# A GLA mixer with a convolutional FFN on one core: state tiles of their own, the first block's heads a unit later, token sums moved to the last block, the last LayerNorm read back inside the FFN, and a reordered opening

## Chip, cores and metric

One core of a Trainium2 chip runs the whole kernel. The metric is device time in microseconds (us) of one execution; lower is better. The kernel before takes 2162.0 us, the median of 3 runs (2158.67 to 2163.49).

## What is computed

One decoder layer of the reference: a chunked gated linear attention (GLA) mixer, then a causal ConvFFN, each with a residual, a LayerNorm and an adaLN modulation from the conditioning vector c. S = 2048 tokens, D = 1024, 4 heads of 128 key and 256 value columns, 2816 hidden columns in the FFN. All is float32.

```python
mod = silu(c) @ mod_w + mod_b                     # shift, scale, gate of each sub-layer
h = x * (1 + scale) + shift
q, k, v, r, a_lr = split(h @ w_in)                # GLA
b = cumsum(log_sigmoid(a_lr @ w_a2 + b_a) / 16)   # in chunks of 64 tokens
o = causal(q_dec @ k_inv.T) @ v + q_dec @ state   # per chunk
state = state * exp(b_last) + k_dec.T @ v
o = o * rsqrt(mean(o * o) + eps) * norm_g
x = layer_norm(alpha * x + gate * ((o * silu(r)) @ w_o))
h = x * (1 + scale2) + shift2
x = layer_norm(alpha * x + gate2 * (convffn(h) @ w_down))
```

## The kernel before, in words

Every float32 product is made from three float32r products: an operand is split into a high part (a cast on ACT, L104) and a rest (a subtraction on DVE, L107), and `mm3` issues high x high, high x rest, rest x high (L110, L111, L112). These three lines are nearly all of TensorE's (PE's) work.

The mixer runs over four blocks of 512 tokens (tb 0 to 3). A block is 32 *units*; a unit is one 1 MB split weight tile `hl` and 24 matmuls of 512 columns. Units 0 to 3 make v for heads 0 and 1, 4 to 7 q and k of these heads, 8 to 11 the gate r; 12 to 23 repeat this for heads 2 and 3; 24 to 31 are the output projection. Weights come as `raw` loads on the SP queue and are split two units ahead, some are stored split (`wq_d`) and loaded back in later blocks. In the last block all come split, so neither ACT nor DVE has a weight to split there.

The rest of the mixer is cut into steps that `at_unit` hangs on a unit and `tick` runs in the order in which they were hung. A head has four: `head_a` (four transposes of k, L635, evicted as `KTt`; then two banks of `ps_w<-Q,KI` attention products, read by DVE's masked copies L649, L650), `head_b` (state updates: products into a bank, DVE's L676 or L678 into `S32[:, h]`, split into `Shl`), `head_c` (output products `v,at` and `Shl,Q` into two banks of 12 matmuls each; ACT squares L704, POOL's power L170/L171, ACT's `on` L710 reads the bank again), `head_d` (transposes L718 and the gate L720). Before, the registering loops put all `head_a` ahead of `head_c`, so that where both hang on one unit (head 1's a with head 0's c, head 3's a with head 2's c) a comes first. Each head's state lives in one slice of one tile, so that the next update of a head overwrites what the split of the last one reads.

PSUM has eight banks: four under the tag "mm" for the long products (`ps_mm`) and four under "w" (`ps_w`), taken in turn by every head step, transpose group and small product. A matmul into a bank waits until its last reader there is done.

Three further places are touched. The **opening**: PE spins on a constant tile (L400; 62, 4 and 18 matmuls) while the modulation sums run (eight rows, 0 to 7, accumulated on DVE, L226/L231; row 7 of the first pair on ACT, L239, and PE, L242; `mod_fin`, L253 to L258), until `make` (L518, L520) has the first modulated x split into `xm`. `x_pre` (L284 to L298) loads four 512 KB tiles, makes four differences of token quarters for the FFN's seven Strassen-like products and stores them; it is called twice in tb 2 for the first half of the tokens (units 4 and 13) and twice in the FFN for the second (steps 6 and 9). The **hand-off** to the FFN: the last block's normalised rows `z` (L778) stay in SBUF as `zs_last`, and `start_rest` transposes all of them (32 transposes, L759, evicted by ACT as `xt`, L764) between the products of FFN step 0. The FFN then has 2 x 22 steps of seven products each, and a down-projection follows. In step 0 the third product adds to the bank of the first, which ACT must have copied out as `p1` (L948) before.

## Time and profile before

| | |
|---|---|
| median of 3 runs | 2162.0 us |
| the profiled execution | 2164.01 us |
| its span | 2162.3 us |
| busy: PE, DVE, ACT, POOL | 99%, 67%, 41%, 6% |
| chain that ended last | PE 92%, DVE 3%, ACT 2%, DMA 2%, issue 1% |
| granted TensorE clock, mean | 0.994 |

How to read it: PE's busy share is an average over the span, and its rest is the waits that the view of waits lists by releaser. A matmul is pipelined, so its own duration overlaps the next one's; the step from start to start is what it costs. The granted clock is 1.00 or 0.50 of full speed in a stretch (2.4 or 1.2 GHz).

### The profile page before, as it was taken

What the parts mean: (1) busy time and instruction counts of PE and PEld (TensorE: products, weight loads), DVE (VectorE), ACT (ScalarE), POOL (GpSimd) and SP (SyncE); (2) the same over time, 40 slices, a digit from 0 to 9 for tenths busy, and PEclk for the clock granted to TensorE, in tenths of its full rate; (3) what the DMA queues carried; (4) which work ended last, traced back from release to release, by engine and by line L of the source; (5) the groups of instructions that cost most, each with busy time, mean ns of one, the idle gap of its engine ahead of it and who ended that gap; (6) DMA issues with size and microseconds to landing.
All of it is one profiled execution on the core that took longest, in us unless ns stands there. A gap on an engine that the chain in (4) does not pass through costs nothing.

```text
span 2162.3 us, 26743 instructions
## 1 busy us (share of the span) xinstructions
PE 2135.5 (99%) x9924; PEld 1780.3 (82%) x9924; DVE 1456.6 (67%) x2031; ACT 886.2 (41%) x1333; POOL 134.5 (6%) x298
## 2 busy tenths in 40 slices
PE   9899999999999999999999999999999999999998
PEld 8788888888888888788888888888888888888887
DVE  6788666667443444688777778766666797578556
ACT  3545443443342333544444445333333443344333
POOL 0111101010001000100000000000000000021002
PEclk9999999999999999999999999999999999999999
DMA  7387547589756546687545558877777797577562
GB/s 298 120 286 287 172 176 265 205 315 359 252 195 246 187 166 230 247 324 275 185 178 204 182 194 319 311 251 275 259 266 264 269 327 278 185 240 258 193 204 88
DMA packets 150211, 515.66 MB, mean 238 GB/s; under 512 B 17120, under 2 KB 17248, under 8 KB 132160
## 3 DMA queue, kind: packets, MB, share of 16 engines
q1 hardware_dynamic: 150080, 513.94, 66.7%
q8 instruction: 78, 1.28, 0.2%
q14 instruction: 53, 0.43, 0.1%
HBM read 351.09 MB, written 162.79 MB: 238 GB/s over the span
## 4 chain that ended last, share of the span: by engine, by line
PE 92%; DVE 3%; ACT 2%; DMA 2%; issue 1%; POOL 0%; SPq 0%; DVEq 0%; POOLq 0%; ACTq 0%
PE ps_mm L110 22%; PE ps_mm L112 22%; PE ps_mm L111 22%; PE ps_w L110 8%; PE ps_w L111 8%; PE ps_w L112 8%; DMA xs<-xt_d 1%; PE ps_w L400 1%; PE ps_w L718 1%; DMA raw<-in_wab_dram 1%; PE ps_w L759 0%; DVE hl L107 0%; PE ps_w L487 0%; ACT hl L104 0%; PE ps_w L488 0%
## 5 line engine op out<-in xcount | busy, mean ns | idle before, releaser
L110 PE MATMUL ps_mm<-xc,hl 128*128 128x512 f32 x704 | 274.3, 390 | 1.7 <-ACT p L948 1.0
L112 PE MATMUL ps_mm<-xc,hl 128*128 128x512 f32 x704 | 274.0, 389 | 0.2 <-DVE hl L107 0.2
L111 PE MATMUL ps_mm<-xc,hl 128*128 128x512 f32 x704 | 273.8, 389 | 0.0
L110 PE MATMUL ps_mm<-xm,hl 128*128 128x512 f32 x496 | 195.1, 393 | 0.3 <-ACT hl L104 0.3
L112 PE MATMUL ps_mm<-xm,hl 128*128 128x512 f32 x496 | 193.6, 390 | 1.6 <-DVE hl L107 1.6
L111 PE MATMUL ps_mm<-xm,hl 128*128 128x512 f32 x496 | 193.7, 391 | 0.0
L110 PEld LDWEIGHTS ps_mm<-xc,hl 128*128 128x128 f32 x704 | 132.1, 188 | 30.1 <-ACT p L948 1.7
L112 PEld LDWEIGHTS ps_mm<-xc,hl 128*128 128x128 f32 x704 | 132.1, 188 | 28.0 <-DVE hl L107 0.6
L111 PEld LDWEIGHTS ps_mm<-xc,hl 128*128 128x128 f32 x704 | 132.1, 188 | 27.3
L962 DVE SCALAR_TENSOR_TENSOR ct<-U,cw_sb,ct 128x512 f32<-128x512 f32 x176 | 131.7, 748 | 19.2 <-ACT ct L956 17.7
L104 ACT CAST hl<-raw 128x1024 fp32r<-128x1024 f32 (+1 forms) x91 | 89.5, 983 | 130.8 <-PE ps_mm L112 54.3
L107 DVE TENSOR_TENSOR hl<-raw,hl 128x1024 fp32r<-128x1024 f32 (+1 forms) x91 | 103.4, 1138 | 56.7 <-ACT hl L104 56.2
L110 PE MATMUL ps_w<-xc,hl 128*128 128x512 f32 x352 | 137.0, 389 | 0.4 <-ACT xt L764 0.4
L111 PE MATMUL ps_w<-xc,hl 128*128 128x512 f32 x352 | 136.9, 389 | 0.0
L112 PE MATMUL ps_w<-xc,hl 128*128 128x512 f32 x352 | 136.9, 389 | 0.0
L104 ACT CAST dhl<-raw 128x1024 fp32r<-128x1024 f32 x57 | 60.1, 1054 | 163.7 <-PE ps_mm L112 103.2
L107 DVE TENSOR_TENSOR dhl<-raw,dhl 128x1024 fp32r<-128x1024 f32 x57 | 69.6, 1221 | 69.4 <-ACT dhl L104 69.4
L112 PEld LDWEIGHTS ps_mm<-xm,hl 128*128 128x128 f32 x496 | 93.3, 188 | 21.7 <-DVE hl L107 2.0
L110 PEld LDWEIGHTS ps_mm<-xm,hl 128*128 128x128 f32 x496 | 93.5, 189 | 19.1 <-ACT hl L104 0.8
L111 PEld LDWEIGHTS ps_mm<-xm,hl 128*128 128x128 f32 x496 | 93.4, 188 | 17.9
L110 PE MATMUL ps_mm<-dhl 128*128 128x512 f32 x264 | 102.7, 389 | 0.0
L111 PE MATMUL ps_mm<-dhl 128*128 128x512 f32 x264 | 102.7, 389 | 0.0
(239 smaller groups left out, 4979.0 us busy)
## 6 DMA issues: line engine op xcount, KB each, us to landing
hl<-wq_d SPq DMA_DIRECT2D x64, 1024.0 KB, 4.8
hc_d<-ct SPq DMA_DIRECT2D x154, 256.0 KB, 2.6
raw<-hc_d SPq DMA_DIRECT2D x70, 512.0 KB, 4.3
draw<-wc_d SPq DMA_DIRECT2D x70, 512.0 KB, 4.9
raw<-in_wab_dram SPq DMA_DIRECT2D x64, 512.0 KB, 5.2
wq_d<-hl SPq DMA_DIRECT2D x32, 1024.0 KB, 4.9
wu<-in_wup_dram SPq DMA_DIRECT2D x44, 512.0 KB, 4.3
wg<-in_wup_dram SPq DMA_DIRECT2D x44, 512.0 KB, 3.6
```

Source lines behind the costliest of these rows:

```text
L104: accs["copy"] = nc.scalar.copy(h, src)
L107: return nc.vector.tensor_tensor(l, src if lsrc is None else lsrc, h.bitcast(F32), op=ALU.subtract)
L110: nc.tensor.matmul(po, a[0], b[0], start=first, stop=False, skip_group_check=resumed)
L111: nc.tensor.matmul(po, a[0], b[1], start=False, stop=False, skip_group_check=resumed)
L112: return nc.tensor.matmul(po, a[1], b[0], start=False, stop=last, skip_group_check=resumed)
L400: mm = nc.tensor.matmul(pm[:, 256:512], still[:, 0:P], still, start=True, stop=True)
L718: nc.tensor.transpose(pt[:, s * P:s * P + P], on[:, s, e * P:e * P + P], ident)
L962: nc.vector.scalar_tensor_tensor(ct, U[:, o + i:o + i + 512], cw_sb[:, j, i:i + 1], ct, op0=ALU.mult, op1=ALU.add)
```

## The change

- **State tiles.** Each state update writes a tile of its own out of eight (tag "S"), not the head's slice of `S32`.
- **Heads.** In tb 0 all head steps come one unit later. One loop now hangs all four steps of a head, so that in every block `head_c` of head 0 comes ahead of `head_a` of head 1 in their common unit, and the same for heads 2 and 3.
- **Modulation sums** of the second sub-layer: the same 16 pieces in tb 0, six of the last seven one to three units later; `mod2` at unit 28.
- **x_pre** of the first half: from tb 2 (units 4, 13) to tb 3 (units 3, 14); the first one of the second half from FFN step 6 to 7.
- **Last LayerNorm.** `start_rest` makes no transposes. Step 1 of the FFN loads the four stored tiles `z` again, steps 2 to 5 transpose and evict two column groups each.
- **Opening.** Spins of 64 and 13 in a bank of their own; all eight rows of the first sum on DVE; both first weight casts ahead of the first `xraw` on ACT; ACT makes row 0 of the later sums; `waw` in one copy and one subtraction.

```diff
@@ -28,7 +28,7 @@
 HALF = 1024
 NP = NJ // 2
 AHEAD = 2
-SPIN = (62, 4, 18)
+SPIN = (64, 13)
 KEEP = [2] * 10 + [1] * 4 + [0] * 10 + [1] * 8
 ALPHA = 2.0 ** 0.25
 EPS = 1e-5
@@ -207,7 +207,11 @@
     def mod_row(raws, dk):
         return raws[dk // 2].rearrange("p (k d c) -> p k d c", k=2, d=2)[:, :, dk % 2]
 
-    def mod_cols(s, pr, qs, raws=None, by_act=False, after=None, rows=range(KT)):
+    def mod_row1(s, pr, raws, after):
+        accs[s, pr] = t2p.tile([P, 2, 256], F32, tag="t2", name="macc")
+        order(nc.scalar.activation(accs[s, pr], mod_row(raws, 0), AF.Copy, scale=cs[:, 0:1]), after)
+
+    def mod_cols(s, pr, qs, raws=None, rows=range(KT), after=None):
         if raws is None:
             raws = {}
             for q in qs:
@@ -220,42 +224,21 @@
             sc = cs[:, dk:dk + 1]
             if dk == 0:
                 accs[s, pr] = t2p.tile([P, 2, 256], F32, tag="t2", name="macc")
-                if by_act:
-                    order(nc.scalar.activation(accs[s, pr], wk, AF.Copy, scale=sc), after[0])
-                else:
-                    i = nc.vector.tensor_scalar(accs[s, pr], wk, sc, None, op0=ALU.mult)
-                    if after is not None:
-                        order(i, after[1])
+                i = nc.vector.tensor_scalar(accs[s, pr], wk, sc, None, op0=ALU.mult)
             else:
                 acc = accs[s, pr]
-                accs["last"] = nc.vector.scalar_tensor_tensor(acc, wk, sc, acc, op0=ALU.mult, op1=ALU.add)
-                if dk == 1 and by_act:
-                    order(accs["last"], accs["hl"])
-
...
-    def mod_fin(s, pr, pm=None):
+                i = accs["last"] = nc.vector.scalar_tensor_tensor(acc, wk, sc, acc, op0=ALU.mult, op1=ALU.add)
+            if after is not None:
+                order(i, after)
+                after = None
+
+    def mod_fin(s, pr):
         acc = accs.pop((s, pr))
-        o = md[:, s, 2 * pr:2 * pr + 2]
-        b = mbs_sb[:, s, 2 * pr:2 * pr + 2]
-        if pm is None:
-            pm = psum("w", 4)
-        else:
-            i = nc.vector.tensor_tensor(o, pm[:, 4:8].rearrange("p (k c) -> p k c", k=2), b, op=ALU.add)
-            order(i, accs["last"])
-            b = o
+        pm = psum("w", 4)
         for c in range(4):
             mm = nc.tensor.matmul(pm[:, c:c + 1], acc[:, c // 2, c % 2 * P:c % 2 * P + P], one, start=True, stop=True)
-        return mm, nc.vector.tensor_tensor(o, pm[:, 0:4].rearrange("p (k c) -> p k c", k=2), b, op=ALU.add)
+        return mm, nc.vector.tensor_tensor(md[:, s, 2 * pr:2 * pr + 2], pm[:, 0:4].rearrange("p (k c) -> p k c", k=2),
+                                           mbs_sb[:, s, 2 * pr:2 * pr + 2], op=ALU.add)
 
...
-        pm0 = psum("w", 4)
-        spin(SPIN[0], pm0)
-        mod_cols(0, 0, range(4), start[0][0], rows=range(7))
-        acc_last = accs["last"]
-        spin(SPIN[1], pm0, mod_rows_act(start[0][0], (7,), pm0))
+        ps_spin = psum("mm", 4)
+        spin(SPIN[0], ps_spin)
+        mod_cols(0, 0, range(4), start[0][0])
 
         load(ba_sb, ba)
         load(ng_sb, ng)
         waw = ab.tile([P, KT, 96], F32R, name="waw")
 
         def make_waw(after):
-            for r in range(3):
-                order(nc.scalar.copy(waw[:, :, r * 32:r * 32 + 16], war), after)
-                nc.vector.tensor_tensor(waw[:, :, r * 32 + 16:r * 32 + 32], war,
-                                        waw[:, :, r * 32:r * 32 + 16].bitcast(F32), op=ALU.subtract)
+            wv = waw.rearrange("p k (r c) -> p k r c", r=3)
+            wb = war[:, :, None, :].to_broadcast([P, KT, 3, 16])
+            order(nc.scalar.copy(wv[:, :, :, 0:16], wb), after)
+            nc.vector.tensor_tensor(wv[:, :, :, 16:32], wb, wv[:, :, :, 0:16].bitcast(F32), op=ALU.subtract)
 
...
-        S32 = ab.tile([P, NH, DV], F32, name="S32")
+        state = [None] * NH
         Shl = [None] * NH
 
         def mod2():
@@ -505,43 +486,45 @@
 
             xm = []
 
-            def acc(pr):
-                mod_cols(0, pr, range(4), start[pr][0], pr == 1, (done[0], done[1 if pr == 1 else 2]))
-
-            def make(pr):
-                mm, i = mod_fin(0, pr, pm0 if pr == 0 else None)
+            def make(pr, then=None):
+                mm, i = mod_fin(0, pr)
                 if pr == 0:
-                    spin(SPIN[2], pm0, mm)
+                    order(i, accs["hl"])
+                    spin(SPIN[1], ps_spin, mm)
                 for kt in (2 * pr, 2 * pr + 1):
                     r = start[pr][1][:, kt % 2 * 512:kt % 2 * 512 + 512]
                     if kt == 1:
-                        nc.vector.tensor_scalar(r, r, md[:, 0, kt, 1:2], md[:, 0, kt, 0:1], op0=ALU.mult, op1=ALU.add)
+                        i = nc.vector.tensor_scalar(r, r, md[:, 0, kt, 1:2], md[:, 0, kt, 0:1], op0=ALU.mult, op1=ALU.add)
                     else:
                         nc.scalar.activation(r, r, AF.Identity, bias=md[:, 0, kt, 0:1], scale=md[:, 0, kt, 1:2])
+                    if kt == 1:
+                        fw.append(unit())
+                        order(accs["hl"], i)
                     t = act_tile("xm")
                     sub = split(t[:, 0], t[:, 1], r)
                     xm.append(t)
-                return accs["copy"], sub, i
+                return sub
 
             fw.append(unit())
             done = make(0)
-            accs["last"] = done[1]
-            fw.append(unit())
-            make_waw(done[1])
+            mod_row1(0, 1, start[1][0], accs["copy"])
+            accs["last"] = done
+            make_waw(done)
             issue(3)
             for pr in range(4):
                 if pr < 3:
                     load_unit()
                     if pr < 2:
                         start_loads(pr + 2)
-                    acc(pr + 1)
+                        mod_row1(0, pr + 2, start[pr + 2][0], accs["copy"])
+                    mod_cols(0, pr + 1, range(4), start[pr + 1][0], range(1, KT), accs["hl"] if pr == 0 else mod_done)
+                    mod_done = accs["last"]
                 for po, w in ((pq, fw[0]), (pk, fw[1])):
                     wv = w.rearrange("p s (k c) -> p s k c", k=KT)
                     for kt in (2 * pr, 2 * pr + 1):
                         mm3(po, (wv[:, 0, kt], wv[:, 1, kt]), (xm[kt][:, 0], xm[kt][:, 1]), kt == 0, kt == KT - 1)
                 if pr < 3:
-                    done = make(pr + 1)
-                    accs["last"] = done[1]
+                    accs["last"] = make(pr + 1)
                 mm_a(pa, xm, (2 * pr, 2 * pr + 1))
                 if pr == 2:
                     make_w2s()
@@ -672,13 +655,14 @@
                     if H["last"] and s == 3:
                         continue
                     po = pst[:, i * DV:i * DV + DV]
-                    if H["S"][s] is None:
-                        nc.vector.tensor_copy(S32[:, h], po)
+                    old, new = state[h], ab.tile([P, DV], F32, tag="S", name="S", bufs=8)
+                    if old is None:
+                        nc.vector.tensor_copy(new, po)
                     else:
-                        nc.vector.scalar_tensor_tensor(S32[:, h], S32[:, h], el[:, 1, s:s + 1], po,
-                                                       op0=ALU.mult, op1=ALU.add)
+                        nc.vector.scalar_tensor_tensor(new, old, el[:, 1, s:s + 1], po, op0=ALU.mult, op1=ALU.add)
+                    state[h] = new
                     st1 = ab.tile([P, 2, DV], F32R, tag="Shl", name="Shl", bufs=8)
-                    split(st1[:, 0], st1[:, 1], S32[:, h])
+                    split(st1[:, 0], st1[:, 1], new)
                     Shl[h] = st1
                     if i == 0:
                         H["S"][-1] = st1
@@ -752,15 +736,13 @@
                     store(zn_d[tb * 4 + t], zs[t])
             tick()
 
-        def ln1_out(tb, zs, kts, after=None):
+        def ln1_out(tb, zs, kts, by_act=False):
             for kt in kts:
                 pt = psum("w", 4)
                 for t in range(4):
-                    tr = nc.tensor.transpose(pt[:, t * P:t * P + P], zs[t][:, kt * P:kt * P + P], ident)
-                    if after is not None:
-                        order(tr, after)
+                    nc.tensor.transpose(pt[:, t * P:t * P + P], zs[t][:, kt * P:kt * P + P], ident)
                 xt = t2p.tile([P, TB], F32, tag="t2", name="xt")
-                if after is not None:
+                if by_act:
                     nc.scalar.activation(xt, pt, AF.Identity, bias=B2[:, kt:kt + 1], scale=A2[:, kt:kt + 1])
                 else:
                     nc.vector.tensor_scalar(xt, pt, A2[:, kt:kt + 1], B2[:, kt:kt + 1], op0=ALU.mult, op1=ALU.add)
@@ -803,30 +785,27 @@
             gated = []
             Hs = [dict(h=h, last=last, gated=gated) for h in range(NH)]
             for i, u in ((0, 6), (1, 8), (2, 18), (3, 20)):
-                at_unit(b + u, head_a, Hs[i])
-                at_unit(b + u + 1, head_b, Hs[i])
-            for i, u in ((0, 8), (1, 10), (2, 20), (3, 22)):
-                at_unit(b + u, head_c, Hs[i])
-            for i, u in ((0, 10), (1, 12), (2, 22), (3, 24)):
-                at_unit(b + u, head_d, Hs[i])
+                u += b + (tb == 0)
+                for k, f in ((0, head_a), (1, head_b), (2, head_c), (4, head_d)):
+                    at_unit(u + k, f, Hs[i])
             at_unit(b + 12, next_decays, (2, 3))
             if tb == 0:
                 load(lnc, lncol)
                 for k in range(8):
                     at_unit(8 + k, gate_step, 0, k, gs1)
                 at_unit(16, gate_end, 0, G1, gs1)
-                for i, u in enumerate((14, 14, 15, 15, 16, 16, 16, 17, 17, 18, 19, 20, 21, 22, 23, 24)):
+                for i, u in enumerate((14, 14, 15, 15, 16, 16, 16, 17, 17, 17, 18, 21, 23, 24, 25, 26)):
                     at_unit(u, mod_cols, 1, i // 4, (i % 4,))
                     if i % 4 == 3:
                         at_unit(u + 1, mod_fin, 1, i // 4)
-                at_unit(26, mod2)
+                at_unit(28, mod2)
...
-            if tb == 2:
-                at_unit(b + 4, x_pre, 0, 0)
-                at_unit(b + 13, x_pre, 0, 1)
+            if tb == 3:
+                at_unit(b + 3, x_pre, 0, 0)
+                at_unit(b + 14, x_pre, 0, 1)
...
-            if last:
-                zs_last = zs
-            else:
+            if not last:
                 xm = nxt["xm"]
...
-        def start_rest(last_mm):
-            ln1_out(NTB - 1, zs_last, range(8), last_mm)
+        def start_rest():
             for i in (3, 2):
                 x_fill(ur, X0, i, x_stage(up, 0, i))
 
         nextx, ahead_x = list(PROD), []
-        todo = {6: [(x_pre, 1, 0)], 9: [(x_pre, 1, 1)]}
+        zl = []
+
+        def ln1_last(n):
+            if n == 0:
+                for t in range(4):
+                    zl.append(z_tile())
+                    load(zl[-1], zn_d[4 * (NTB - 1) + t])
+            else:
+                ln1_out(NTB - 1, zl, range(2 * n - 2, 2 * n), True)
+
+        todo = {n + 1: [(ln1_last, n)] for n in range(5)} | {7: [(x_pre, 1, 0)], 9: [(x_pre, 1, 1)]}
         G2 = gp.tile([P, D], F32, tag="G", name="G2")
         load(G2, G2_d)
         prev = None
@@ -1089,7 +1075,7 @@
             else:
                 nc.gpsimd.tensor_copy(U[:, 0:2], halo[:, j])
             if n == 0:
-                start_rest(mm)
+                start_rest()
             add(nc.vector, U[:, 2:514], pb, p1)
             st["h0"] = conv_a(U, 0, j)
             if Wn is not None:
```

How the order changes, at three places. First PE in tb 1 where head 1's `head_a` and head 0's `head_c` share a unit (rows of the same kind cut; `KI_2829` of before and `KI_2828` of the change are the same tile). Before:

```order
L635 MATMUL ps_w<-ident,KI_2829 128x128 x4
L110 MATMUL ps_w<-Q,KI 128x192
L111 MATMUL ps_w<-Q,KI 128x192
L112 MATMUL ps_w<-Q,KI 128x192
L110 MATMUL ps_w<-v,at 128x256
L111 MATMUL ps_w<-v,at 128x256
L112 MATMUL ps_w<-v,at 128x256
L110 MATMUL ps_w<-Shl,Q 128x256
```

Now:

```order
L110 MATMUL ps_w<-v,at 128x256
L111 MATMUL ps_w<-v,at 128x256
L112 MATMUL ps_w<-v,at 128x256
L110 MATMUL ps_w<-Shl,Q 128x256
L111 MATMUL ps_w<-Shl,Q 128x256
L112 MATMUL ps_w<-Shl,Q 128x256
L618 MATMUL ps_w<-ident,KI_2828 128x128 x4
L110 MATMUL ps_w<-Q,KI 128x192
```

The 24 output products of head 0 now stand right ahead of head 1's transposes and its attention products, in the same turn of the four "w" banks.

Second, DVE at the state updates of head 3 in tb 0. Before:

```order
L678 SCALAR_TENSOR_TENSOR S_400<-S_400,el,ps_w 128x256
L231 SCALAR_TENSOR_TENSOR macc<-mraw,cs,macc 128x512
L107 TENSOR_TENSOR Shl<-S_400,Shl 128x256
L374 TENSOR_TENSOR raw<-raw,G_279 128x1024
L678 SCALAR_TENSOR_TENSOR S_400<-S_400,el,ps_w 128x256
```

Now:

```order
L660 COPY S<-ps_w 128x256
L240 TENSOR_TENSOR md<-ps_w,mbs_sb 128x4
L662 SCALAR_TENSOR_TENSOR S<-S,el,ps_w 128x256
L107 TENSOR_TENSOR Shl<-S,Shl 128x256
L662 SCALAR_TENSOR_TENSOR S<-S,el,ps_w 128x256
```

An update no longer stands behind the subtraction of the one before it with other work between them, and the `macc` and `raw` work left this place.

Third, ACT at the hand-off (`z` are the last block's rows, `p` and `u` the copies of the first products). Before:

```order
L778 ACTIVATE z<-z,rs 128x1024 x2
L104 CAST hl<-wu 128x1024
L104 CAST xc<-xs 128x512 x2
L948 COPY p_7731<-ps_mm 128x512
L104 CAST hl<-wg 128x1024
L764 ACTIVATE xt<-ps_w,B_107,A_106 128x512 x3
```

Now:

```order
L760 ACTIVATE z<-z,rs 128x1024 x2
L104 CAST hl<-wu 128x1024
L104 CAST xc<-xs 128x512 x2
L925 COPY p_7774<-ps_mm 128x512
L104 CAST hl<-wg 128x1024
L104 CAST hl<-wu 128x1024
L925 COPY u_7837<-ps_mm 128x512
```

What stands ahead of `p` is the same; the evictions `xt` behind it are gone from here, and on PE so are the 32 transposes (L759).

## Rows read from the trace of the kernel before

**Rows 1.** The page, part 1 (busy us, share, instructions of each engine).

```profile
PE 2135.5 (99%) x9924; PEld 1780.3 (82%) x9924; DVE 1456.6 (67%) x2031; ACT 886.2 (41%) x1333; POOL 134.5 (6%) x298
```

**Rows 2.** Waits of PE: what waited, releaser, us in all, times, longest.

```profile
PE ps_w L110 <- DVE S L678: 6.5, 3, 3.0
...
PE ps_mm L110 <- ACT u L948: 1.9, 3, 0.7
...
PE ps_w L110 <- DVE KTt L107: 0.6, 1, 0.6
```

**Rows 3.** Windows: us, busy us (xcount) of PE, PEld, DVE, ACT, POOL, PEclk, DMA, GB/s.

```profile
14.00:20.80 6.80, 6.54 (x27) 5.98 (x26) 5.43 (x10) 5.17 (x9) 0.00 (x0) 0.50 1.05 401
31.05:34.46 3.41, 3.31 (x8) 2.40 (x9) 3.41 (x5) 1.51 (x3) 0.00 (x0) 0.50 1.05 407
89.08:95.90 6.82, 5.70 (x24) 5.54 (x25) 6.14 (x12) 3.60 (x10) 1.91 (x2) 0.50 0.39 136
177.82:181.24 3.42, 3.42 (x18) 3.42 (x18) 3.22 (x7) 1.48 (x6) 0.46 (x1) 0.50 0.84 323
700.00:860.00 160.00, 160.00 (x825) 136.59 (x824) 68.25 (x120) 55.24 (x119) 9.38 (x22) 1.00 0.52 192
886.00:930.00 44.00, 39.55 (x182) 30.88 (x181) 31.46 (x45) 29.33 (x38) 5.59 (x14) 1.00 0.84 304
```

**Rows 4.** Timeline of PE: start, us, line, operation, [idle before <- releaser].

```profile
18.66 0.63 PE L110 MATMUL ps_w<-xm,hl 128*128 128x512 f32 x1
...
86.29 0.35 PE L110 MATMUL ps_w<-Q,KI 128*128 128x192 f32 x1 [1.71 <-DVE S L678]
...
90.20 0.55 PE L110 MATMUL ps_w<-v,at 128*128 128x256 f32 x1 [2.99 <-DVE S L678]
...
177.56 0.38 PE L110 MATMUL ps_w<-v,at 128*128 128x256 f32 x1 [1.85 <-DVE S L678]
...
511.35 0.50 PE L112 MATMUL ps_mm<-xm,hl 128*128 128x512 f32 x1 [1.60 <-DVE hl L107]
```

**Rows 5.** Opening: SP's second weight load, ACT rows; DMA part of 0:32 (last, landing).

```profile
5.65 0.43 SPq L125 DMA_DIRECT2D raw<-in_wab_dram  x1
...
11.28 1.05 ACT L104 CAST hl<-raw 128x1024 fp32r<-128x1024 f32 x1 [0.45 <-DMA raw<-in_wab_dram]
...
14.64 0.81 ACT L520 ACTIVATE xraw<-xraw,md 128x512 f32<-128x512 f32 x1 [2.31 <-DVE md L258]
...
raw<-in_wab_dram SPq DMA_DIRECT2D x7, 512.0 KB, 8.1
```

**Rows 6.** Timelines around a head_c: ACT, POOL and PE in tb 2; POOL in tb 0.

```profile
625.26 0.38 ACT L704 ACTIVATE sq<-ps_w 128x256 f32<-128x256 f32 x1 [0.83 <-PE ps_w L112]
...
627.37 0.84 ACT L710 ACTIVATE on<-ps_w,ss 128x256 f32<-128x256 f32 x2 [1.13 <-POOL ss L171]
...
626.63 0.71 POOL L171 TENSOR_TENSOR ss<-ss,mhalf 128x2 f32<-128x2 f32 x1
...
623.63 0.28 PE L110 MATMUL ps_w<-v,at 128*128 128x256 f32 x1
...
626.50 1.04 PE L718 MATMUL ps_w<-ident,on 128*128 128x128 f32 x8
...
93.97 1.60 POOL L171 TENSOR_TENSOR ss<-ss,mhalf 128x2 f32<-128x2 f32 x1
```

**Rows 7.** Timeline of DVE: the four differences of x_pre in tb 2.

```profile
504.50 5.00 DVE L290 TENSOR_TENSOR xp<-xp 128x1024 f32<-128x1024 f32 x4
```

**Rows 8.** Timelines at the hand-off: ACT, then PE.

```profile
895.96 0.57 ACT L948 COPY p<-ps_mm 128x512 f32<-128x512 f32 x1
...
891.64 0.39 PE L112 MATMUL ps_mm<-xc,hl 128*128 128x512 f32 x1
...
894.13 1.64 PE L759 MATMUL ps_w<-ident,z 128*128 128x128 f32 x13 [1.18 <-ACT z L778]
...
896.59 0.50 PE L110 MATMUL ps_mm<-xc,hl 128*128 128x512 f32 x1 [0.82 <-ACT p L948]
```

More of the change, by code (lines that the diff above doesn't have):

```diff
@@ L230, in mod_cols @@
                 acc = accs[s, pr]
-                accs["last"] = nc.vector.scalar_tensor_tensor(acc, wk, sc, acc, op0=ALU.mult, op1=ALU.add)
-                if dk == 1 and by_act:
-                    order(accs["last"], accs["hl"])
-    def mod_rows_act(raws, rows, pm):
-        parts = []
-        for dk in rows:
-            parts.append(t2p.tile([P, 2, 256], F32, tag="t2", name="mpart"))
-            nc.scalar.activation(parts[-1], mod_row(raws, dk), AF.Copy, scale=cs[:, dk:dk + 1])
-        for c in range(4):
-            for n, part in enumerate(parts):
-                mm = nc.tensor.matmul(pm[:, 4 + c:5 + c], part[:, c // 2, c % 2 * P:c % 2 * P + P], one,
-                                      start=n == 0, stop=n == len(parts) - 1)
-        return mm
```

## The prediction

> **What bounds the kernel now.** Read the page's part 1 first: PE is busy in 99% of the span [rows 1], so the kernel is bound by PE, and DVE, ACT and POOL matter only where PE waits for one of them. That leaves two sources of a gain, the 27 us in which PE is not busy and the stretches at half clock. So the view of PE's waits comes next [rows 2]: the reader is to see how small the list is, and that its largest entry, 6.5 us in three waits, is DVE's state update L678. Third, the windows [rows 3]: 0.50 in the clock column marks four stretches at half clock (1.2 GHz), of 6.80, 3.41, 6.82 and 3.42 us; a stretch busy with matmuls loses half its length there. Last, PE's timeline gives each wait its place [rows 4]. Some 27 us of waits and about half of 20.5 us at half clock are all that can be won; whatever the change moves on DVE, ACT or SP outside these places costs nothing as long as PE has its operands.
>
> The sum is made against the profiled execution, 2164.0 us, which lies 2.0 us above the median shown; the forecast is brought to the median at the end. Two times closer than 0.2% (4.3 us) can't be told apart here.
>
> **Opening.** Before, the first real matmul starts at 18.66 [rows 4], behind `xraw` on ACT at 14.64, which waited for the two-step `md` [rows 5]. Now ACT does both weight casts first. The second weight load is issued at 5.65 and takes 8.1 us by the median of these loads, so it lands near 13.75; a cast takes 1.05 (11.28 row), so `xraw` starts near 14.8, ends at 15.6 by its 0.81, and the first cast of `xm` lets PE start near 16.2: 2.45 us earlier [rows 5]. How much of it is worth something hangs on the clock: it is 0.50 up to 20.80 [rows 3], and if it stays so, matmuls in the 2.45 us gained run at half speed, worth 1.25. Bounds: 0.8 (the load lands half a microsecond late) and 2.45 (the clock rises as much earlier as the real work starts). Nothing here tells the two apart, and I take the middle, **-1.8**. The 3.41 us at half clock from 31.05 on, and the wait for `xm` there, stay, because the DMA share there is 1.05 [rows 3]: loads set that place, and none is removed.
>
> **Heads of tb 0 and the state tiles.** The three waits for L678 are 1.71, 2.99 and 1.85 us, 6.55 together, and the first matmul behind a wait lasts longer as the pipeline refills (0.50 at 511.35 [rows 4] against 0.39 at 891.64 [rows 8]), so some 0.1 more each, 6.9 in all. With tiles of its own an update needs only its bank and the last state, no longer the subtraction that reads the old slice; with the steps a unit later it also has left the `macc` work. I take all three as gone: -6.9. Two half-clock stretches lie around them [rows 3]. In 89.08 to 95.90 PE is busy 5.70 us at half speed, so half of it, 2.85, comes back less a little at the edges, where the pipeline hides some, 2.7; in 177.82 to 181.24 half of 3.42, 1.7. In all -6.9 - 2.7 - 1.7 = **-11.3**. The smaller end is -6.9 (the clock falls all the same).
>
> **What the new order of the steps adds.** The rows on PE's order show that head 0's 24 output products now stand right ahead of head 1's transposes and attention products. In turn they take banks po0, po1, transposes, attention 0, attention 1 out of four, so attention 1 needs po0's bank, and that is free only when ACT's `on` has read it. The chain after po0's last matmul is square, POOL power, `on`: from 625.26 to 628.21 (627.37 + 0.84), 2.95 us [rows 6]. PE fills it with 12 matmuls of 256 columns (half of the 24 between 623.63 and 626.50, 1.44 us), four transposes (half of the eight up to 627.29, 0.4) and six short products (at most 0.12 each, 0.7), less the pipeline's overlap about 2.3 us. The rest, **0.7 us**, is a new wait, at each of seven places (two in each of tb 0, 2 and 3, one in tb 1; in the other pair of tb 1 ten long matmuls stand between). At three places it is longer. Head 1 of tb 0 is the first POOL power of the program, 1.60 us at 93.97 where the one at 626.63 takes 0.71 [rows 6], and part of a weight cast stands between: 0.7 + 0.9 + 0.8 = 2.4, and 1.0 more as the clock may fall. Where a weight cast (1.05 [rows 5]) stands between the squares it is 0.7 + 0.95 = 1.65 (tb 1); in tb 0's second pair the cast is only in part in the way, 0.9. Sum: 2.4 + 1.0 + 0.9 + 1.65 + 4 x 0.7 = **+8.75**. Below, it is nothing if ACT is quicker; above, each place has the 1.60 us power. Behind a waiting `on`, ACT's next casts queue, and the `Shl` casts of the next head wait with them; these are needed two units later.
>
> **Moved pieces.** The later modulation sums hold raw tiles longer, and the weight load behind them comes later: +0.5 (0 to 2). `x_pre` leaves tb 2: DVE's four differences fill 504.50 to 509.50 [rows 7], and PE then waits 1.60 us for the weight split queued behind them [rows 4]; with the wait for `KTt` close behind it (0.6 [rows 2]) and 0.1 each of refill, **-2.4**. In tb 3 the same 5 us stand in a block without weight splits, where DVE is busy 68 of 160 us [rows 3]: +0.5 (0 to 2); the eight loads on SP are behind pre-split weights there, two units ahead. The small waits of tb 1 are left as they are.
>
> **Hand-off.** Before, PE fills the wait for `p`, from 891.9 (the last product starts at 891.64) to 896.59 [rows 8], with 16 of the 32 transposes, 1.75 us at 0.11 each (1.64 for 13, with the drain); the rest of the 4.7 is wait. What ACT has ahead of `p` (895.96) is unchanged, so now PE stands still until 896.6: **4.5 us in one piece** less the pipeline's end. The 16 transposes are paid later: +1.75. Gone are waits behind them for `u`, 1.9 [rows 2], and refill and a few tenths for `xt`: the whole window has 44.00 - 39.55 = 4.45 us without PE [rows 3], of which some 2.4 lie ahead of 896.59, so 2.05 and six refills of 0.1, -2.6. After an idle of 1.85 us at 177.56 [rows 4] a half-clock stretch of 3.42 us followed [rows 3], so one is taken here too: +1.7. Sum **+0.85**; bounds -1 (the clock holds) and +4 (two such stretches, and the waits for `u` stay in part). Before, the idle pieces here were short and the window's clock is 1.00 [rows 3].
>
> The Trainium skill, "TensorE: Matmul & The Clock Gate", section "Why this matters for your kernels", says to leave no longer idle between bursts of matmuls, else the engine falls back to half rate. By that rule the hand-off is where this change loses, and the trace agrees in its row at 177.56, so the 1.7 us stay in the sum; were the rule left out and the clock held, the sum would be 1.7 lower.
>
> **Sum.** -1.8 - 11.3 + 8.75 + 0.5 - 2.4 + 0.5 + 0.85 = -4.9, so 2159.1 for a profiled execution like this one, and 2.0 less against the median: **2157.1 us**, about 0.2% faster.
>
> **Rivals.**
>
> *The new order is free.* If the square-power-on chain ends before PE comes back to the bank (ACT idle at that point, as at 625.26), the 8.75 us are not paid: 2157.1 - 8.75 = 2148.4. For it: the surplus is only 0.7 us of 2.95 at four of the seven places. Against it: three places have a cast or the long power in the chain.
>
> *The bank wait takes the place of the state wait (the other side).* With the 1.60 us power at every place, the chain is 3.85 us and each wait 1.6; an idle of that kind can halve the clock for 3.42 us, 1.7 lost. Seven times 3.3 is 23.1 in place of 8.75: 2171.5. With the clock falling at half of the places it is 2165.5. It decides from about 0.7 us more per place on, where the 4.9 are used up. For it: 1.85 us at 177.56 brought the clock down. Against it: 1.60 at 511.35 did not, and later powers are short.
>
> *The hand-off and the opening give nothing back.* If the idle of 4.5 us costs two half-clock stretches (1.7 more), and half of the later waits stay (1.3), with no gain at the opening (1.8): 2157.1 + 4.8 = 2161.9, no change that can be told. For it: ACT stays the late engine there, with 29.33 of 44.00 us busy [rows 3]. Against it: eight `xt` evictions leave ACT.
>
> *The state waits only move.* L678's late end in tb 0 is DVE's queue (6.14 of 6.82 us busy [rows 3]), not the slice. If the steps meet the same queue a unit later, half of the 11.3 stays: 2162.7.
>
> **How the numbers follow.** Forecast 0.46 (its own range 2152 to 2161), order free 0.19, hand-off and opening 0.10, state waits only move 0.12, bank wait 0.13. Faster by over 0.2% needs less than 2157.7: the order free, 0.19, 0.30 of the forecast, whose unsure terms (opening, hand-off, the clock at head 1) were mostly taken on the dear side, and 0.05 of the two rivals near 2162 where the order costs less beside them: 0.54. Within 0.2%: 0.16 of the forecast, 0.15 of these two, 0.01 of the bank wait: 0.32. Slower: 0.12 of the bank wait and 0.02 of these two, 0.14. The range takes in the order being free, and the bank wait with the clock falling at half of the places: 2147 to 2166.
>
> **What would show it.** In the waits of PE, L678's successor is gone or under 1 us, and a new entry "`ps_w` <- ACT `on`" of 5 to 8 us stands at attention products of every block. Half clock is gone at 89 and 178 us. The hand-off shows one idle of about 4.5 us released by ACT `p`, and half clock behind it. The first real matmul starts near 16.2. I'm wrong if `on` releases much more than 9 us, if the state updates still stand in the list, or if the wait near 511 has only moved to tb 3.

## The result and the profile after

The changed kernel takes 2173.42 us (median of 5 runs, 2169.91 to 2181.06), the kernel before 2162.76 (5 runs): a ratio of 1.0058, 95% interval 1.0036 to 1.0079. It is 0.6% slower, where a little faster was forecast, and outside the range. The profiled execution of the change is the slowest of its five, 2181.06 us, 17 us above that of before; the terms below are read from it, so they sum to 17 and not to the 11 us between the medians.

Its page (part 1):

```profile
PE 2141.0 (98%) x9909; PEld 1784.2 (82%) x9909; DVE 1455.4 (67%) x2027; ACT 887.7 (41%) x1332; POOL 134.7 (6%) x298
```

PE's waits now, by releaser (in us, times, longest):

```profile
PE ps_w L110 <- ACT on L694: 12.3, 8, 2.9
PE ps_w L239 <- DVE macc L230: 5.6, 3, 3.7
PE ps_mm L110 <- ACT p L925: 4.1, 1, 4.1
PE ps_w L618 <- DVE KI L601: 3.0, 2, 2.1
PE ps_w L110 <- ACT xm L104: 2.3, 2, 1.3
...
PE ps_w L702 <- ACT on L694: 1.2, 1, 1.2
```

The 6.5 us of waits for state updates [rows 2] are gone, as forecast. In their place stands ACT's `on`, 12.3 us in eight waits, and two entries that the forecast had at 0.5 us each: `mod_fin`'s matmuls (L239) behind `macc`, and the transposes of k (L618) behind `KI`. (Of L239's 5.6 us, 1.7 stand in the opening, at 12.27; of L618's 3.0, 0.9 stood there before as well, in tb 0.) The single 4.1 us behind `p` is the hand-off. Where the waits stand, in PE's timeline (the last three behind `on`, 0.58, 0.52 and 0.58 at 621.92, 756.84 and 836.83, are not shown):

```profile
93.07 0.53 PE L110 MATMUL ps_w<-Q,KI 128*128 128x192 f32 x1 [2.88 <-ACT on L694]
...
180.72 0.36 PE L110 MATMUL ps_w<-Q,KI 128*128 128x192 f32 x1 [2.63 <-ACT on L694]
...
226.29 0.37 PE L239 MATMUL ps_w<-ones,macc 128*128 128x1 f32 x1 [3.71 <-DVE macc L230]
...
318.31 0.53 PE L110 MATMUL ps_w<-Q,KI 128*128 128x192 f32 x1 [1.99 <-ACT on L694]
...
401.60 0.35 PE L110 MATMUL ps_w<-Q,KI 128*128 128x192 f32 x1 [1.05 <-ACT on L694]
...
539.62 0.36 PE L110 MATMUL ps_w<-Q,KI 128*128 128x192 f32 x1 [2.02 <-ACT on L694]
...
737.23 0.30 PE L618 MATMUL ps_w<-ident,KI 128*128 128x128 f32 x1 [2.09 <-DVE KI L601]
...
912.99 0.80 PE L110 MATMUL ps_mm<-xc,hl 128*128 128x512 f32 x1 [4.14 <-ACT p L925]
```

And windows at half clock (columns as in [rows 3]), which come with the waits:

```profile
92.96:96.37 3.41, 3.30 (x11) 2.92 (x12) 1.99 (x5) 2.04 (x7) 0.95 (x2) 0.50 0.66 245
181.71:185.12 3.41, 3.41 (x9) 2.64 (x8) 3.31 (x7) 2.24 (x6) 0.92 (x2) 0.50 0.73 263
226.08:232.91 6.83, 6.62 (x20) 5.56 (x21) 6.83 (x12) 2.15 (x3) 0.00 (x0) 0.50 0.65 216
318.24:321.65 3.41, 3.34 (x11) 2.95 (x12) 1.70 (x4) 1.99 (x7) 0.94 (x2) 0.50 0.98 299
403.57:406.99 3.42, 3.42 (x10) 2.66 (x9) 2.17 (x5) 0.28 (x1) 0.00 (x0) 0.50 0.44 161
540.10:543.52 3.42, 3.42 (x11) 2.84 (x11) 2.58 (x6) 1.47 (x4) 0.86 (x2) 0.50 0.06 24
738.08:741.49 3.41, 3.41 (x14) 3.12 (x14) 2.32 (x5) 1.42 (x2) 0.00 (x0) 0.50 1.03 417
912.16:918.98 6.82, 5.99 (x14) 4.75 (x15) 6.75 (x10) 3.14 (x5) 0.00 (x0) 0.50 0.85 295
```

Before, two such stretches lay between 80 us and the hand-off [rows 3]; now there are seven, and one at the hand-off. Each begins at or within two microseconds of the end of a wait in the list above. The stretch from 31.05 on that stood before is missing here, though the wait near 30 us is still there (1.31 us).

Where the time went is read from the start of the same matmul in both timelines (after less before, us):

| place | difference | what lies between |
|---|---|---|
| first real matmul | -2.4 | opening |
| first product of v, heads 2 and 3, tb 0 | -5.5 | state waits gone, 2.9 behind `on` |
| first output projection, tb 0 | -4.1 | state wait gone, 2.6 behind `on` |
| end of tb 0 | +3.0 | 3.7 behind `macc`, 6.83 us at half clock |
| end of tb 1 | +10.2 | 2.0 and 1.05 behind `on`, twice 3.4 us at half clock, 1.2 at L702 (0.6 before) |
| end of tb 2 | +11.4 | -2.5 by x_pre, 2.0 and 0.6 behind `on`, half clock |
| end of tb 3 | +16.8 | 2.1 behind `KI`, half clock, 0.5 and 0.6 behind `on` |
| FFN, after some five steps | +17.3 | hand-off and the moved transposes |
| end | +17.0 | |

### The profile page after: what moved, and what is told of

The parts are those of the page before. It is cut to its first block, busy times and chain, and to the rows that moved or that the text cites. A ratio compares the mean times of both kernels' runs of the same rounds, so it can differ in the third digit from the quotient of the medians.

```text
span 2179.4 us, 26712 instructions
## 1 busy us (share of the span) xinstructions
PE 2141.0 (98%) x9909; PEld 1784.2 (82%) x9909; DVE 1455.4 (67%) x2027; ACT 887.7 (41%) x1332; POOL 134.7 (6%) x298
## 4 chain that ended last, share of the span: by engine, by line
PE 89%; DVE 4%; DMA 2%; ACT 2%; issue 2%; POOL 1%; SPq 0%; DVEq 0%; POOLq 0%; ACTq 0%
PE ps_mm L110 21%; PE ps_mm L112 21%; PE ps_mm L111 21%; PE ps_w L110 8%; PE ps_w L111 7%; PE ps_w L112 7%; DMA raw<-in_wab_dram 1%; PE ps_w L743 1%; PE ps_w L702 1%; DVE hl L107 0%; POOL ss L171 0%; ACT hl L104 0%; DMA xp<-xm_d 0%; ACT on L694 0%; PE ps_w L468 0%
## 5 line engine op out<-in xcount | busy, mean ns | idle before, releaser
L110 PE MATMUL ps_mm<-xm,hl 128*128 128x512 f32 x496 | 197.3, 398 | 0.0
L111 PE MATMUL ps_mm<-xm,hl 128*128 128x512 f32 x496 | 196.4, 396 | 0.0
L112 PE MATMUL ps_mm<-xm,hl 128*128 128x512 f32 x496 | 196.0, 395 | 0.0
L112 PEld LDWEIGHTS ps_mm<-xm,hl 128*128 128x128 f32 x496 | 95.0, 192 | 20.1
L110 PEld LDWEIGHTS ps_mm<-xm,hl 128*128 128x128 f32 x496 | 95.4, 192 | 19.0
L111 PEld LDWEIGHTS ps_mm<-xm,hl 128*128 128x128 f32 x496 | 95.0, 192 | 18.5
```

The costliest lines, as they stand in the source:

```text
L110: nc.tensor.matmul(po, a[0], b[0], start=first, stop=False, skip_group_check=resumed)
L111: nc.tensor.matmul(po, a[0], b[1], start=False, stop=False, skip_group_check=resumed)
L112: return nc.tensor.matmul(po, a[1], b[0], start=False, stop=last, skip_group_check=resumed)
```

## Experiments

All times are medians; ratios are to the kernel before on the same chip, whose medians in the three sets of runs were 2162.83, 2161.57 and 2162.32 us. So a difference between versions of two sets is uncertain by about 1 us.

**The order of head_c and head_a.** The theory was that the new order's bank wait is the whole loss. First the change with that order alone undone:

```diff
-                for k, f in ((0, head_a), (1, head_b), (2, head_c), (4, head_d)):
-                    at_unit(u + k, f, Hs[i])
+                at_unit(u, head_a, Hs[i])
+                at_unit(u + 1, head_b, Hs[i])
+            for k, f in ((2, head_c), (4, head_d)):
+                for i, u in ((0, 6), (1, 8), (2, 18), (3, 20)):
+                    at_unit(b + (tb == 0) + u + k, f, Hs[i])
```

> The changed kernel with one thing undone: all head_a and head_b are hung on their units ahead of all head_c and head_d again (tb 0 still one unit later). Theory (bank wait): the eight waits of attention products for ACT's `on`, 12.3 us in the profile of the changed kernel, and the half-clock stretches behind five of them (8.5 us) go, so 2152 to 2158 us, and no wait of `ps_w<-Q,KI` for `on` is listed. Rival (the state waits were only covered by the bank waits): DVE's state updates stand in the list of PE's waits again with some 6 us, and the time is 2165 to 2170.

2158.72 us, ratio 0.9979 (0.9969 to 0.9989), 14.7 us less than the change. The head of its list of PE's waits:

```profile
PE ps_mm L110 <- ACT p L928: 5.7, 1, 5.7
PE ps_w L110 <- ACT xm L104: 3.0, 2, 1.5
PE ps_mm L110 <- DVE z L732: 2.4, 1, 2.4
```

No `on` and no state update: the rival, that the bank waits only covered the state waits, falls. What is new is 2.4 us behind `z` at 217 us (below). Then the opposite, the new order alone on the kernel before:

```diff
-                at_unit(b + u, head_a, Hs[i])
-                at_unit(b + u + 1, head_b, Hs[i])
...
+                for k, f in ((0, head_a), (1, head_b), (2, head_c), (4, head_d)):
+                    at_unit(b + u + k, f, Hs[i])
```

> The kernel before with only the loop that hangs the head steps written as in the change (c of one head ahead of a of the next in a common unit), no shift, no state tiles. Theory (bank wait): the waits for `on` come at seven or eight places, 8 to 13 us, with half clock behind some, less what the state waits of tb 0 give back (up to 11): 2166 to 2180. Rival (the order by itself is free, it hurts only with the shifted heads): 2160 to 2164.

2173.81 us, ratio 1.0049 (1.0035 to 1.0063): 11 us slower by a reordered loop.

```profile
PE ps_w L110 <- ACT on L710: 7.5, 7, 2.1
```

Not all of the 11 us are these waits: the state updates left its list, and 3.3 us behind the casts and splits of `Shl`, 2.4 us behind a weight cast and 2.1 us of `on` at L277 came into it.

That it is the bank, and not the order as such, was tested by leaving the change as it is and giving the attention products banks of the other tag:

```diff
-                pa = psum("w", 4)
+                pa = psum("mm", 4)
                 pav = pa[:, 0:384].rearrange("p (s c) -> p s c", s=2)
```

> The changed kernel as it is, c ahead of a, with the two attention banks of each head taken from the mm banks instead of the w banks. Theory (the wait is for the bank of head_c's first output, nothing else in the order): the waits of the attention products for `on` go, 12.3 us, with the half clock behind them, 8.5 us; the late modulation sums stay (up to 7 us): 2156 to 2160. Rival (it is the order, head_c ahead of transposes, whatever the bank): waits of the same size appear at the transposes or the long products: 2168 to 2174.

2155.84 us, ratio 0.9972 (0.9963 to 0.9981), 17.6 us less than the change, with output products, transposes and attention products still one behind the other at the same eight places (in the second pair of tb 1 the ten long matmuls between them moved behind). In its list `on` releases no attention product any more, and the windows at the two pairs of tb 0 are at full clock and full:

```profile
PE ps_mm L110 <- ACT p L925: 6.1, 1, 6.1
PE ps_w L239 <- DVE macc L230: 5.5, 3, 3.7
```

```profile
85.00:110.00 25.00, 25.00 (x149) 22.19 (x148) 19.91 (x33) 14.91 (x37) 4.31 (x6) 1.00 0.66 227
170.00:200.00 30.00, 30.00 (x175) 26.44 (x175) 22.13 (x36) 16.14 (x40) 4.38 (x8) 1.00 0.65 244
```

The late `macc` (5.5 us) stays, as expected. So the mechanism is shown: the attention products of the next head waited for a bank that `head_c`'s output held until ACT's second reading of it. At seven places it is attention 1, the seventh of the twelve short products, as forecast. At the eighth, the second pair of tb 1 (401.60), it is the first of them, behind the ten long matmuls; the forecast had no wait there, and why attention 0 waits there is open.

**The modulation sums.** The schedule of before in the change, and then in the version with a ahead of c:

```diff
-... (14, 14, 15, 15, 16, 16, 16, 17, 17, 17, 18, 21, 23, 24, 25, 26)
+... (14, 14, 15, 15, 16, 16, 16, 17, 17, 18, 19, 20, 21, 22, 23, 24)
-                at_unit(28, mod2)
+                at_unit(26, mod2)
```

> The changed kernel with the units of the second modulation sums as they were before (mod2 at unit 26). Theory: the wait of mod_fin's matmuls for `macc` (3.7 us at 226 us) and the 6.8 us at half clock behind it come from the later schedule, so both go, 7 us where the runs show them as the profile does: 2166 to 2168. Rival: DVE is late there for another reason (the heads a unit later), and the wait stands at another mod_fin: 2172 to 2174.

2170.80 us (2168.23 to 2172.57), ratio 1.0031 (1.0019 to 1.0042). The wait at 226 us is gone, but 0.7 us at L239 at 182 us are new, and 6.8 us at half clock stand there; its runs overlap the change's, and the median lies between the two expectations, so the gain is not settled by this run.

> The changed kernel with both undone, the head loop (a ahead of c) and the units of the second modulation sums. Theory: with a ahead of c, 2158.7 us, PE still waited 2.4 us for `z` at 217 us with 3.4 us at half clock behind it, because the late sums fill DVE there; this goes with the old units, about 4 to 5 us: 2153 to 2155. Rival (DVE is late there for the shifted heads): no difference, 2158 to 2159.

2151.64 us, ratio 0.9948 (0.9935 to 0.9962): 7.1 us less than with a ahead of c alone (5.8 us if each is taken against the kernel before of its own set), more than the 4 to 5 expected. The wait behind `z` went as well. The reason is in the change's DVE timeline ahead of 226 us, where the sums stand between weight splits and folds of the gate:

```profile
223.69 0.75 DVE L230 SCALAR_TENSOR_TENSOR macc<-mraw,cs,macc 128x512 f32<-128x512 f32 x1
224.35 1.22 DVE L357 TENSOR_TENSOR raw<-raw,G 128x1024 f32<-128x1024 f32 x1
225.49 0.74 DVE L230 SCALAR_TENSOR_TENSOR macc<-mraw,cs,macc 128x512 f32<-128x512 f32 x1
```

The last sum ends at 226.23, and PE goes on at 226.29. Output projection units have weights to fold and to split on DVE; three of the sums now stand in them, one before.

**x_pre.** Back in tb 2 (units 4 and 13), in the change:

> The changed kernel with x_pre of the first half back in tb 2, units 4 and 13. Theory: the wait for `KI` at 737 us (2.1 us) and its 3.4 us at half clock come from x_pre's four differences on DVE and go (-4.0), and the waits near 511 us come back (+2.5 to +3.0, perhaps with half clock, +1.7): 2172 to 2174, no difference. Rival: the differences also delay things that the list does not show, then 2168 or less.

2170.50 us (2169.57 to 2177.21), ratio 1.0036 (1.0024 to 1.0049); the wait at 737 us went and two of 1.3 and 0.7 us came in tb 2, where one behind `on` (2.0 us) went as well; its runs overlap the change's, so it settles nothing on the time. In tb 3 the reason is the order on DVE in the change:

```profile
731.35 0.68 DVE L597 TENSOR_TENSOR KI<-ps_mm,E 128x512 f32<-128x512 f32 x1
731.95 3.73 DVE L273 TENSOR_TENSOR xp<-xp 128x1024 f32<-128x1024 f32 x3
735.60 0.68 DVE L107 TENSOR_TENSOR KI<-KI,KI 128x512 fp32r<-128x512 f32 x1
736.39 0.69 DVE L601 TENSOR_TENSOR KI<-KI,el 128x512 f32<-128x512 f32 x1
```

Three of the four differences stand between the product `KI` and its split and scaling, 3.7 us; L618 waits for the end of the last row. Later units, in the version of 2151.64:

```diff
-                at_unit(b + 3, x_pre, 0, 0)
-                at_unit(b + 14, x_pre, 0, 1)
+                at_unit(b + 12, x_pre, 0, 0)
+                at_unit(b + 15, x_pre, 0, 1)
```

> The version with a ahead of c and the old units of the modulation sums (2151.6 us), with the two x_pre of the first half at units 12 and 15 of tb 3 instead of 3 and 14. Theory (the wait for `KI` at 712 us, 1.7 us, comes from the four differences standing ahead of KI on DVE in units 4 and 5): that wait goes and the time is 1 to 2 us less, 2150. Rival (the differences meet head 2's q and k in units 16 to 19 in the same way): a wait of that size stands there, 2151 to 2154.

2149.63 us (2148.76 to 2151.75), ratio 0.9948 (0.9934 to 0.9962), the lowest median of this study and 0.5% under the kernel before. The wait of 1.7 us at 712 is gone, L618's waits are down from 3.1 to 1.1:

```profile
PE ps_mm L110 <- ACT p L928: 4.1, 1, 4.1
...
PE ps_w L618 <- DVE KI L601: 1.1, 2, 0.9
```

Against the version without it the ranges of runs overlap, so the step itself is seen in the trace, not in the time.

**State tiles and shift.** Each alone on the kernel before, and both, with a ahead of c (the diffs are the parts of the change's own diff):

> The kernel before with only the state tiles. Theory (the state waits came from the one slice: an update waits for the split that reads it): the three waits for state updates shrink to a third and the half clock at 89 and 178 us goes, 6 to 10 us: 2153 to 2157. Rival (the waits came from DVE's queue around the updates, so the shift of the heads is what helps): 2160 to 2163.

2163.74 us, ratio 1.0005 (0.9996 to 1.0014): nothing. The state waits shrink only from 6.5 to 4.0, half clock at 85 us stays, and a wait of 2.6 us for `KI` in tb 2 is new, with half clock behind it:

```profile
PE ps_w L110 <- DVE S L679: 4.0, 3, 2.6
PE ps_w L635 <- DVE KI L618: 3.5, 2, 2.6
```

> The kernel before with only the heads of tb 0 a unit later (a ahead of c, one state slice per head). Theory (the state updates were late for DVE's queue in those units, the modulation sums and gate sums of tb 0, and the slice costs little): the waits for state updates at 86, 90 and 177 us go and the half clock with them, up to 11 us: 2152 to 2156. Rival (both are needed, as the state tiles alone gave nothing): 2159 to 2163 with state waits in the list.

2156.66 us, ratio 0.9976 (0.9966 to 0.9985). Two waits of 1.87 and 1.25 us are left, with no half clock behind them:

```profile
PE ps_w L110 <- DVE S L678: 3.1, 2, 1.9
```

> The kernel before with the state tiles and the heads of tb 0 a unit later, a ahead of c, nothing else. Theory (both together take the state waits away): 2152 to 2155, the same as or up to 2 us under the shift alone. Rival (the later modulation sums of the change are needed as well, or the shift meets the same queue): 2159 to 2163.

2156.76 us, ratio 0.9976 (0.9967 to 0.9985), 1.8 us above the range expected. The state waits are gone from the list. From 62 us to the first output projection of tb 0, by the starts of the same matmuls, the tiles alone gain 2.4 us, the shift alone 6.1, both 9.8; but everything comes earlier, and in tb 2 x_pre now meets `KI` (2.3 us, with 3.4 us at half clock behind it) instead of a weight split (1.6 us):

```profile
PE ps_w L635 <- DVE KI L618: 3.2, 2, 2.3
```

So the shift is the part that pays. What the tiles add in tb 0 is not seen in the time: in the profiles some 1 us of it goes by the end of tb 0, 2 us at that collision and 1 more at the hand-off, where this execution has 6.8 us at half clock and the shift alone none.

**The hand-off.** The version of 2151.64 with the last LayerNorm as before (`zs_last` kept, 32 transposes in FFN step 0, and the second half's first x_pre in step 6 again), and with the read-back but p1 copied by DVE:

```diff
-            return t, nc.scalar.copy(t, po)
+            if dve:
+                return t, nc.vector.tensor_copy(t, po)
+            return t, nc.scalar.copy(t, po)
...
-            p1, _ = keep(pa, "p1")
+            p1, _ = keep(pa, "p1", n == 0)
```

> As the one with both undone, and the last LayerNorm kept in SBUF and transposed in FFN step 0 as before. Theory: the single idle of 5.7 us at the hand-off and its 6.8 us at half clock cost more than the later waits and the hidden transposes give, by some 2 us: 2 us faster than that kernel. Rival (the read-back pays): 1 to 3 us slower than that kernel.

2150.78 us (2149.42 to 2152.79), ratio 0.9948 (0.9933 to 0.9963): the same as with the read-back, 2149.65 to 2152.49. The windows of 45 us around the hand-off, first with the LayerNorm as before, then with the read-back:

```profile
870.00:915.00 45.00, 39.80 (x184) 31.22 (x183) 31.43 (x45) 29.14 (x38) 5.50 (x13) 1.00 0.81 295
```

```profile
876.00:921.00 45.00, 40.86 (x170) 33.16 (x169) 35.10 (x48) 27.20 (x36) 5.67 (x12) 0.92 0.75 286
```

Many short waits at full clock on the one side, one long wait and 6.8 us at half clock on the other; the transposes saved here are paid later.

> As the one with both undone, with the read-back kept, but the copy p1 of the first FFN step made by DVE instead of ACT. Theory: what holds PE at the hand-off is ACT's queue ahead of p1 alone (four z, two casts); DVE is free from about 886.5, so the 5.7 us of waiting and the 3.4 us lost at half clock behind it go: 5 to 9 us faster than that kernel, 2145 to 2149. Rival (the next operand, the casts of wu and xs on ACT, is as late): the wait only moves to those and 0 to 3 us are gained.

2151.51 us (2148.68 to 2151.57), ratio 0.9945 (0.9932 to 0.9959). The rival came true. DVE's copy, ACT's queue and PE:

```profile
879.13 0.68 DVE L929 COPY p<-ps_mm 128x512 f32<-128x512 f32 x1
```

```profile
879.30 1.24 ACT L760 ACTIVATE z<-z,rs 128x1024 f32<-128x1024 f32 x1 [0.27 <-POOL rs L759]
880.45 1.03 ACT L104 CAST hl<-wu 128x1024 fp32r<-128x1024 f32 x1
```

```profile
881.53 0.80 PE L110 MATMUL ps_mm<-xc,hl 128*128 128x512 f32 x1 [4.13 <-ACT hl L104]
```

The copy is ready at 879.8, yet PE waits 4.13 us, now for the cast of `wu`, which stands behind the same four `z` on ACT. That the wait is as long as before is chance: in this execution the first `z` began 2.49 us after the first FFN product, in the version of 2151.64 0.96 us after it. In ACT's queue `p` would have come behind the two casts of `xs` (which end at 882.52) and its own 0.57 us, so some 1.5 us after the cast of `wu` (an estimate from these rows): the copy on DVE shortens the wait by that much, and the times do not show it. Late `z` also stand behind the hand-off waits of 5.7 and 6.1 us above (2.54 and 2.88 us after the first FFN product).

## Why the prediction was wrong

- *State waits and shift, -11.3*: right in kind. The waits are gone; tiles and shift together gave 9.8 us in tb 0, 6.1 of them by the shift alone. Both parts act on the waits: the tiles alone left 4.0 of 6.5 us, the shift alone 3.1. But behind what the tiles left the clock fell at 85 us, and behind what the shift left it did not, in these profiles. The half clock at 89 and 178 us that this term gave back stands again at 93 and 182, now with `on`; its price is in the next term. That the rest is DVE's queue around the updates is argued from the order of its work, not tested by itself.
- *The new order, +8.75*: the step that failed. Place and mechanism were right at seven of eight places (attention 1 in po0's bank, until `on`), the size was not. The waits were 12.3 us, above the 9 that the prediction named as a sign of being wrong, and with some 0.15 of refill each 13.5, against 7.75; and half clock came with five of them, 5 x 1.7 = 8.5 us, against 1.0. Together 22.0 in this profile, the slowest of five; by the medians the order costs 14.7 (undone) to 17.6 us (other banks), still well over 8.75. The rival "the bank wait takes the place of the state wait" had 23.1 and 2171.5, close to the measured 2173.4, but by luck: it has a power of 1.60 us at each place, and of the eight powers ahead of these waits one took 1.60, one 1.04 and six 0.71 or 0.72; and 7 us of the loss are the modulation sums'.

  Five waits came near their forecast (2.88 us at 93 for 2.4, 1.99 at 318 for 1.65; 0.58, 0.52 and 0.58 for 0.7 each). Three did not: 2.63 at 180 for 0.9, 2.02 at 539 for 0.7, and 1.05 at 401 for nothing. The prediction took the chain of 2.95 us from a place where ACT was free [rows 6]. At 539 us the squares stood behind a table load and a gate:

```profile
534.50 1.28 ACT L609 ACT_TABLE_LOAD   x1
...
536.29 0.38 ACT L688 ACTIVATE sq<-ps_w 128x256 f32<-128x256 f32 x1
...
538.73 0.84 ACT L694 ACTIVATE on<-ps_w,ss 128x256 f32<-128x256 f32 x2 [1.10 <-POOL ss L171]
```

  and at 180 us `on` stood behind a weight cast that itself waited for DVE:

```profile
178.88 1.04 ACT L104 CAST hl<-raw 128x1024 fp32r<-128x1024 f32 x1 [2.31 <-DVE raw L357]
179.83 0.83 ACT L694 ACTIVATE on<-ps_w,ss 128x256 f32<-128x256 f32 x2
```

  So at both places work ahead in ACT's queue made the bank late (at 539 with a power of 1.04 us on top). At 93, 318 and 401 us POOL's step ahead of the power, which the chain of 2.95 us has at 0.2, was longer too (1.33, 0.89 and 0.87 us, each after a pause of POOL of 17 us or more):

```profile
89.13 1.33 POOL L170 TENSOR_SCALAR ss<-ss 128x2 f32<-128x2 f32 x1 [17.22 <-ACT sq L688]
```

  The larger part of the miss is the clock, 7.5 us, against 4.5 of waiting: its price was put on one place, though the prediction had the row for it, 1.85 us followed by half clock.
- *Later modulation sums, +0.5 (0 to 2)*: too small, 5.8 to 7.1 us by the runs with a ahead of c, and 7.1 us in the profile of the change between the first output projection and the end of tb 0. Only the weight load behind them was costed; that `mod_fin`'s matmuls stand in PE's order and wait for the last sum was not.
- *`x_pre`, -2.4 and +0.5*: the first was right (-2.5 in the curve). The second was 3.8, from 2.1 us of waiting and its half clock. DVE's mean of 68 busy of 160 us [rows 3] said nothing about the microsecond ahead of `KI`.
- *Hand-off, +0.85*: the mechanism was right, the sum partly by luck. One idle of 4.14 us stands behind `p` (4.5 forecast), with half clock from 912.16 on, so here the trace agrees with the rule of the Trainium skill, "TensorE: Matmul & The Clock Gate", section "Why this matters for your kernels", to leave no long idle between bursts of matmuls. The row at 177.56, which the prediction took as agreement too, is an idle of only 1.85 us, shorter than those which that rule warns of: there the measurement goes further than the page. With the later waits gone the curve goes from +16.8 to +17.3, +0.5, but the half-clock stretch was 6.82 us, not 3.42. Two other profiles with the same wait and a stretch of 3.41 us (the change with the old sums, and the version of 2149.63) move by -0.6 and -0.7 there, so the other pieces of this sum were some 1.5 us too dear. Of the 1.9 us for `u`, 0.5 stand at 1343 us and not at the hand-off; the sum does not use them.
- *Opening, -1.8*: first matmul at 16.26, as forecast. At 62 us the change stands at -2.3; over all kernels here those with the new opening stand at -1.0 to -3.7 there and those with the old one at 0 to -2.1, so it is worth some 1 us, and no run tried it alone. The wait near 31 us stayed, as forecast, but its half clock did not, in this profile. The stretch of half clock near 14 to 21 us, by which the prediction bounded this term, stands in the profiles of before and of the change and in none of the other twelve.

Taken without the order's term the forecast is 2157.1 - 8.75 = 2148.4; with the order undone the change runs at 2158.7. Without the sums' 0.5 as well it is 2147.9; with the sums put back too it runs at 2151.6, 9.9 us under its kernel before where 14.2 were forecast. So the rest of the change gives some 70% of its forecast. Of the 4 us that lack, the opening (0.8), the state waits (1.5) and `x_pre` in tb 3 (1.7 us of waiting at 712 for 0.5) make some 3.5, by the profiles; the rest is open.

## What to carry to other kernels

When two steps of a rotation of PSUM banks swap places, price the wait by what the releasing engine has in its queue at that place, not by the length of the reader's own chain elsewhere, and look for a free tag: giving the attention products other banks took the whole loss away. A TensorE wait of a microsecond or two inside dense matmuls may cost as much again in half clock (1.7 us behind each of five waits of 1.05 to 2.88 us here), so several small new waits are worse than their sum. Work moved to a block that is idle on average must be placed against the one operand that PE needs next.

## What the runs showed of the hardware that was not expected

The length of a wait alone does not tell whether half clock follows. In the change, 1.05 us at 401.60 (and 0.29 just behind it) was followed by 3.42 us at half clock from 403.57 on. The same two waits at the same place of the change with the old sums were not:

```profile
396.49 0.36 PE L110 MATMUL ps_w<-Q,KI 128*128 128x192 f32 x1 [1.05 <-ACT on L694]
```

```profile
396.00:406.00 10.00, 9.22 (x50) 7.89 (x51) 4.74 (x9) 2.85 (x6) 0.00 (x0) 1.00 0.46 157
```

Nor were they in the change with `x_pre` back or in the kernel before with the new order. The wait of 1.99 us at tb 1's first pair had half clock in three of these four profiles, and the wait of 2.88 us at tb 0's first pair, which the change and the change with the old sums share, had it in the first alone. With the shift alone, a wait of 1.87 us had none:

```profile
90.44 0.36 PE L110 MATMUL ps_w<-v,at 128*128 128x256 f32 x1 [1.87 <-DVE S L678]
```

```profile
90.00:97.00 7.00, 6.56 (x39) 5.90 (x40) 5.98 (x11) 3.79 (x11) 1.12 (x2) 1.00 0.56 196
```

In sum the half clock with the `on` waits cost some 8.5 us in the change, 6.8 with the old sums and 8.5 with `x_pre` back (half the length of the stretches): in these three the total is steadier than its places. What decides at a single wait is open. Between the opening and the last microseconds the stretches came in two lengths, some 3.4 and 6.8 us. And POOL was slower after a long pause, unevenly: after 52.48 us the power took 1.04 us in the change (537.65), where the next took 0.71, but the step ahead of it 0.23; after 51.81 us it was that step that took 0.89 (315.70), and the power 0.71.
